# Two products of each key tile of a hybrid RWKV-7 block, moved from VectorE to GpSimd

## The chip, the cores and the metric

The kernel runs on one core of one Trainium2 chip. The metric is the device time of one execution in microseconds (us); the time of a kernel is the median of its runs. The engines are called as in the profile: PE is TensorE's matrix multiplication and PEld its weight load, DVE is VectorE, ACT is ScalarE, POOL is GpSimd, SP is SyncE, which here only issues the loads of weights.

## The reference

One layer for 512 tokens of width 1024: a normalization, one wide projection into three token mixers (a short convolution, a gated linear recurrence, an RWKV-7 time mixing with 16 heads of 64), their gated sum, an output projection, and an MLP with squared ReLU. The change touches the inputs of the RWKV-7 recurrence. Cut to that:

```python
decay = jnp.exp(-jnp.exp(w_log))
a = jax.nn.sigmoid(rwkv_a0[l] + xa @ rwkv_a2[l])
kk = kk / jnp.maximum(jnp.sqrt(jnp.sum(kk * kk, axis=-1, keepdims=True)), 1e-12)
k = k * (1.0 + (a - 1.0) * rwkv_ka[l])
...
def step(state, inp):                      # scanned over the tokens
    r_t, w_t, k_t, v_t, kk_t, a_t = inp
    sa = jnp.einsum('bhvk,bhk->bhv', state, -kk_t)
    state = (state * w_t[:, :, None, :]
             + sa[..., None] * (kk_t * a_t)[:, :, None, :]
             + v_t[..., None] * k_t[:, :, None, :])
    return state, jnp.einsum('bhvk,bhk->bhv', state, r_t)
```

## The kernel before

The recurrence is done by chunks of 64 tokens. Within a chunk the running product P of the decays is taken as an exponential of a running sum, so that the recurrence becomes matrix products of four scaled tensors: kk times P of the token before, the receptance r times P, kk times a over P, and the key k over P. The first two stand side by side in the tile AR, the last two in BK, each with 128 channels on the partitions and, on the free axis, 8 chunks of two times 64 columns. A product into one half of such a tile therefore reads 512 columns and writes 8 blocks of 64 with a gap of 64 between them.

The 1024 channels are 8 key tiles of 128, two (jj = 0, 1) in each of four groups (g). For a group, `krv` does all of this:

- it projects k and r of each tile (`proj`: 24 wide matmuls, the weight split into a rounded part `whi` and a rest `wlo`, the latter a subtraction on VectorE at L105) and mixes each with the token before (`shift`: a ScalarE copy at L326 and a VectorE instruction at L108, into `ks` and `rs`);
- for each tile it takes the norm of kk over a matmul `pn` and a chain of short VectorE instructions (`rsqrt_rows`, tile `rqq`), the running sum (`cum`, a scan on VectorE, L462), P (`PP`, with the view `Pt` one column on; ScalarE, L466) and the inverse 1/P (`pinv`, ScalarE, L469), and then AR and BK (L470 to L478). The scaled key is `kp`;
- it takes two products `rk` of r and kp, splits them into a rounded part and a rest (the rests of the second go to the buffers of `t_` and `pinv`), sums them over the channels of a head with the matmuls `pb` (L500), multiplies by v into `bv`, and transposes v (`pV`, L508).

Temporary tiles come from a pool by tag with one buffer each ("a1" to "a5", "ks", "rs", "PPt"), so the same buffer serves the next tile. In the profile they read `a`, since the number in the name is left out; in the order they carry a number of their own, as in `a_712`. After `krv`, `amat` multiplies BK by AR for each chunk and head (`pA`, L530), masks the results into `AXt` on VectorE, and transposes BK (`pB`, L552).

GpSimd sets a few columns (the first of PP in each chunk, L464) and issues the transfers that carry AR, BK, AXt and others to DRAM and back in the layout that the recurrence needs (`axd`, `rtd` at L490, `bkd`, `mpd` at L852). Its one piece of arithmetic is a product at the end, `x0f` at L1251.

Beside the groups' work runs filler work (`ab`: the other two mixers), woven in by generators: `weave` takes one step of the group's work under a raised priority, then some steps of the filler. Within that, a scheduler of the framework fixes each engine's order when the program is built, from the priorities and from its own estimate of how long instructions take. An engine then runs its list strictly in order, and waits for semaphores. Only instructions marked with `keep_in_program_order` or issued by `pin` are held in the written order. So an edit of one instruction can move others.

Of the kernel before, what the change touches and what calls it, by code (L numbers as in the profile page):

```python
# [99 lines left out]
def block_kernel(ctx, tc, xt, win, par, mulr, sw, wout, w1, w2, fg, cst, eyes, out):  # L100
    nc = tc.nc
    v, ac, gp, pe, sy = nc.vector, nc.scalar, nc.gpsimd, nc.tensor, nc.sync

    def tt(o, a, b, op):
        return v.tensor_tensor(out=o, in0=a, in1=b, op=op)  # L105

    def stt(o, a, s, b, op0, op1):
        return v.scalar_tensor_tensor(out=o, in0=a, scalar=s, in1=b, op0=op0, op1=op1)  # L108
# [4 lines left out]
    MUL, ADD, SUB, MAX = ALU.mult, ALU.add, ALU.subtract, ALU.max  # L113
# [46 lines left out]
    def split(pool, src, tag, rows=slice(0, P), bufs=None):  # L160
        th, tl = tag if type(tag) is tuple else (tag + "h", tag + "l")
        hi = pool.tile([P, S], F32R, tag=th, name=th, bufs=bufs)
        lo = pool.tile([P, S], F32R, tag=tl, name=tl, bufs=bufs)
        ac.copy(hi[rows], src)
        tt(lo[rows], src, f(hi[rows]), SUB)
        return hi, lo
# [24 lines left out]
    def rsqrt_rows(pool, o, ps, low, scale=1.0):  # L191

        w = pool.tile([P, S], F32, tag="rqw", name="rqw")
        q = pool.tile([P, 3, 16], F32, tag="rqq", name="rqq")
        v.transpose(w, ps)
        wv = w.rearrange("p (b j) -> p b j", j=32)[:, :, 0]
        if scale == 1.0:
            v.tensor_scalar(out=q[:, 0], in0=wv, scalar1=low, scalar2=None, op0=MAX)
        else:
            ts2(q[:, 0], wv, scale, low, MUL, ADD)  # L200
        rsqrt(q[:, 0], q[:, 1], q[:, 2])
        v.transpose(o, q[:, 1].unsqueeze(2).to_broadcast([P, 16, 32]))
# [20 lines left out]
    def bv_tile(q, dt=F32):  # L223
        return sp.tile([P, S], dt, tag=f"bv{q}", name="bv" if dt == F32 else "ml", align_bytes=AL)
# [86 lines left out]
    def proj(name):  # L311
        w = load_w(win[CN[name]])
        t = pp.tile([P, S], F32, tag="pp", name="pp")
        for kt in range(KT):
            wh, wl = wslice(w, kt)
            mm3(t, wh, wl, hh[:, kt], hl[:, kt], start=kt == 0, stop=kt == KT - 1)
            if kt % 2 == 1 and kt < KT - 1:
                yield
        return t
# [5 lines left out]
    def shift(pt, mu, omu, o):  # L325
        ac.activation(o, pt, AF.Copy, scale=omu)  # L326
        stt(o[:, 1:], pt[:, 0:S - 1], mu, o[:, 1:], MUL, ADD)
# [8 lines left out]
    def WP(tag, bufs=1):  # L336
        return pk.tile([P, S], F32, tag=tag, name=tag, bufs=bufs)
# [68 lines left out]
    def load_sw(pool, tag, j, a, n):  # L406
        raw = wp.tile([P, 2, P], F32, tag="swr", name="swr", bufs=2)
        sy.dma_start(raw[:, 0:n], sw[j, :, a:a + n])
        hi = pool.tile([P, n, P], F32R, tag=tag + "h", name=tag + "h", bufs=1)
        lo = pool.tile([P, n, P], F32R, tag=tag + "l", name=tag + "l", bufs=1)  # L410
        ac.copy(hi, raw[:, 0:n])
        m = tt(lo, raw[:, 0:n], f(hi), SUB)
        if tag == "swc":
            tc.keep_in_program_order(m)
        return hi, lo

    def c3(t):
        return t.rearrange("p (c t) -> p c t", c=NC)
# [4 lines left out]
    def krv(g, G_):  # L423
        G_.AR = pk.tile([P, 2, NC, 2, L], F32, tag="AR", name="AR")
        G_.BK = pk.tile([P, 2, NC, 2, L], F32, tag="BK", name="BK")
        vs = [p1.tile([P, S], F32, tag=f"v{h}", name=f"v{h}") for h in range(2)]
        for jj in range(2):
            j = 2 * g + jj
            if j == 0:
                ks, rs = k0, r0  # L430
            else:
                ks, rs = WP("ks"), WP("rs")
                t = yield from proj(("k", j))
                shift(t, pv("mu_k", j), dvp(OMK, j), ks)
            sq = WP("a1")
            ac.activation(sq, ks, AF.Square, scale=pv("kk", j))
            sqh, sql = split(pk, sq, "b")
            yield
            if j:
                t = yield from proj(("r", j))  # L440
                shift(t, pv("mu_r", j), dvp(OMR, j), rs)
            swh, swl = load_sw(pk, "swa", j, 0, 2)
            pw = pc.tile([P, S], F32, tag="pu", name="pw")
            pe.matmul(pw, swh[:, 0], lws, start=True, stop=False)
            pe.matmul(pw, swl[:, 0], lws, start=False, stop=True)
            sig = WP("a1")
            ac.activation(sig, pw, AF.Tanh, bias=pv("w0", j), scale=0.5)
            ac.activation(sig, sig, AF.Identity, bias=one[:, 0:1])
            pa = pc.tile([P, S], F32, tag="py", name="pa")
            pe.matmul(pa, swh[:, 1], las, start=True, stop=False)  # L450
            pe.matmul(pa, swl[:, 1], las, start=False, stop=True)
            av = WP("a4")
            ac.activation(av, pa, AF.Tanh, bias=pv("a0", j), scale=0.5)
            yield
            pn = pm.tile([P, S], F32, tag="pm", name="pn")
            pe.matmul(pn, bd, sqh, start=True, stop=False)
            pe.matmul(pn, bd, sql, start=False, stop=True)
            kk = WP("a5")
            rsqrt_rows(pk, kk, pn, 1e-24)
            stt(kk, ks, pv("kk", j), kk, MUL, MUL)  # L460
            cum = WP("a2")
            v.tensor_tensor_scan(out=cum, data0=smk, data1=sig, initial=0.0, op0=MUL, op1=ADD)  # L462
            PP = pk.tile([P, NC, L + 1], F32, tag="PPt", name="PPt")
            gp.memset(PP[:, :, 0:1], 1.0)  # L464
            Pt = PP[:, :, 1:L + 1]
            ac.activation(Pt, c3(cum), AF.Exp, scale=-0.5 * CW)  # L466
            v.tensor_copy(PL[:, g, jj], PP[:, :, L])
            pinv = WP("a3")
            ac.activation(pinv, cum, AF.Exp, scale=0.5 * CW)  # L469
            stt(G_.AR[:, jj, :, 0], c3(kk), -1.0, PP[:, :, 0:L], MUL, MUL)  # L470
            tt(G_.AR[:, jj, :, 1], c3(rs), Pt, MUL)
            t_ = WP("a1")
            stt(t_, av, 1.0, kk, ADD, MUL)
            stt(G_.BK[:, jj, :, 0], c3(t_), 0.5, c3(pinv), MUL, MUL)
            kp = WP("a2")
            ac.activation(kp, av, AF.Identity, scale=pv("ka", j), bias=dvp(OKA, j))
            tt(kp, kp, ks, MUL)
            tt(G_.BK[:, jj, :, 1], c3(kp), c3(pinv), MUL)  # L478

            if jj == 0:  # L480
                rk = [WP(f"rk{h}") for h in range(2)]
            for h in range(2):
                r = slice(64 * h, 64 * h + 64)
                stt(rk[h][64 * jj:64 * jj + 64], rs[r], part[r, PI["rk"], j:j + 1], kp[r], MUL, MUL)

        for jj in range(2):
            for h in range(2):
                gp.dma_start(axd[0, :, 0:64, g, 2 * h + jj].rearrange("c d t -> d c t"),
                             G_.AR[64 * h:64 * h + 64, jj, :, 0])
            gp.dma_start(rtd[:, :, g, jj].rearrange("c p t -> p c t"), G_.AR[:, jj, :, 1])  # L490
        rk = [split(pk, rk[h], ("a1", "a3") if h else "b") for h in range(2)]
        for h in range(2):
            q = 2 * g + h
            t = yield from proj(("v", q))
            shift(t, pv("mu_v", q), dvp(OMV, q), vs[h])
            yield
        for h in range(2):
            pb = pm.tile([P, S], F32, tag="pm", name="pb")
            for i in range(2):
                pe.matmul(pb, bd, rk[h][i], start=i == 0, stop=i == 1)  # L500
            BV[2 * g + h] = bv_tile(2 * g + h)
            tt(BV[2 * g + h], pb, vs[h], MUL)
        yield
        for b in range(2):
            pt = pm.tile([P, 2, 2, P], F32, tag="pm", name="pV")
            for i in range(2):
                for h in range(2):
                    pe.transpose(pt[:, i, h], vs[h][:, (2 * b + i) * P:(2 * b + i + 1) * P], ident)  # L508
            vt = p1.tile([P, 2, 2, P], F32, tag="vt", name="vt", bufs=2)
            ac.copy(vt, pt)  # L510
            for i in range(2):
                c = 2 * (2 * b + i)
                gp.dma_start(vtd[c:c + 2, :, g].rearrange("c s e v -> (c s) (e v)"),
                             vt[:, i].rearrange("p h x -> p (h x)"))
        yield
# [826 lines left out]
```

## Time and profile before

| | |
|---|---|
| median of 3 runs | 1024.95 us (1024.88 to 1027.47) |
| the profiled execution | 1024.48 us |
| its span, first to last instruction | 1022.7 us |
| mean granted clock of TensorE | 0.997 |
| the groups' work (first `pn` to last `pB`) | about 47 to 394 us |
| VectorE busy from 50 to 100 us | 44.80 us |
| VectorE busy from 130 to 190 us | 46.00 us |
| VectorE busy from 250 to 320 us | 52.81 us |
| VectorE busy from 340 to 405 us | 49.32 us |

The profile shows one execution. "Busy" is the time in which an engine worked on an instruction; a wait is the idle time in front of an instruction, put down to the instruction that ended last among those it waited for ("<-"). A row of a timeline has the start in us from the span's start, the length in us, engine, line, operation, tile written and tiles read, and in brackets the idle time before. In a list of waits each row has the waiting instruction, the releaser, the total in us, how often, and the longest. Successive instructions of one engine overlap somewhat, so the distance of their starts is shorter than their lengths: a wide matmul is listed with 0.39 us, and 150 of them between 15 and 50 us took 35.00 us.

### The profile page before, as it was taken

What the parts mean: (1) busy time and instruction counts of PE and PEld (TensorE: products, weight loads), DVE (VectorE), ACT (ScalarE), POOL (GpSimd) and SP (SyncE); (2) the same over time, 40 slices, a digit from 0 to 9 for tenths busy, and PEclk for the clock granted to TensorE, in tenths of its full rate; (3) what the DMA queues carried; (4) which work ended last, traced back from release to release, by engine and by line L of the source; (5) the groups of instructions that cost most, each with busy time, mean ns of one, the idle gap of its engine ahead of it and who ended that gap; (6) DMA issues with size and microseconds to landing.
All of it is one profiled execution on the core that took longest, in us unless ns stands there. A gap on an engine that the chain in (4) does not pass through costs nothing.

```text
span 1022.7 us, 15725 instructions
## 1 busy us (share of the span) xinstructions
PE 1005.3 (98%) x6110; PEld 817.6 (80%) x6110; DVE 735.9 (72%) x1251; ACT 512.7 (50%) x757; POOL 114.0 (11%) x187
## 2 busy tenths in 40 slices
PE   8999999999999999999999999999999999999997
PEld 5777887888887878888887887888888888888885
DVE  6997597599865876795668778646555546987775
ACT  7765463655544655365446444435333334445354
POOL 1012011201212112201222100110000000000001
PEclk9999999999999999999999999999999999999998
DMA  6443744834546445844777634543323324643452
GB/s 233 125 128 107 191 134 116 220 103 130 147 136 165 125 138 147 268 143 129 209 225 212 187 88 120 174 141 127 94 92 104 102 84 171 222 139 128 144 165 103
DMA packets 50266, 151.28 MB, mean 148 GB/s; under 512 B 6672, under 2 KB 10256, under 8 KB 50192
## 3 DMA queue, kind: packets, MB, share of 16 engines
q1 hardware_dynamic: 34816, 99.93, 30.8%
q0 software_dynamic: 14656, 49.29, 17.8%
q8 instruction: 48, 0.79, 0.3%
q10 hardware_dynamic: 720, 1.05, 0.3%
q14 instruction: 26, 0.21, 0.1%
HBM read 123.52 MB, written 26.74 MB: 147 GB/s over the span
## 4 chain that ended last, share of the span: by engine, by line
PE 84%; DVE 9%; ACT 2%; DMA 2%; issue 2%; SPq 0%; DVEq 0%; ACTq 0%
PE acc L1102 16%; PE pp L169 13%; PE pp L171 12%; PE pp L170 12%; PE p L169 6%; PE p L171 6%; PE p L170 6%; DVE wlo L105 2%; PE acc L169 1%; PE acc L171 1%; PE acc L170 1%; DMA raw<-in_win 1%; PE py L688 1%; DMA xT<-in_xt 1%; PE pu L677 1%
## 5 line engine op out<-in xcount | busy, mean ns | idle before, releaser
L148 ACT CAST whi<-raw 128x1024 fp32r<-128x1024 f32 (+1 forms) x164 | 169.6, 1037 | 251.0 <-PE pp L170 76.3
L105 DVE TENSOR_TENSOR wlo<-raw,whi 128x1024 fp32r<-128x1024 f32 (+1 forms) x176 | 206.7, 1176 | 93.6 <-ACT whi L148 93.1
L169 PE MATMUL pp<-hh,whi 128*128 128x512 f32 x688 | 270.6, 394 | 1.1 <-DVE rs L108 1.1
L170 PE MATMUL pp<-hl,whi 128*128 128x512 f32 x688 | 269.8, 392 | 0.0
L171 PE MATMUL pp<-hh,wlo 128*128 128x512 f32 x688 | 269.7, 392 | 0.0
L169 PEld LDWEIGHTS pp<-hh,whi 128*128 128x128 f32 x688 | 129.2, 188 | 29.0 <-DVE rs L108 1.7
L171 PEld LDWEIGHTS pp<-hh,wlo 128*128 128x128 f32 x688 | 129.2, 188 | 27.4 <-DVE wlo L105 0.3
L170 PEld LDWEIGHTS pp<-hl,whi 128*128 128x128 f32 x688 | 129.2, 188 | 26.6
L169 PE MATMUL p<-h2h,whi 128*128 128x512 f32 x256 | 100.4, 392 | 0.0
L171 PE MATMUL p<-h2h,wlo 128*128 128x512 f32 x256 | 99.7, 389 | 0.0
L170 PE MATMUL p<-h2l,whi 128*128 128x512 f32 x256 | 99.7, 389 | 0.0
L108 DVE SCALAR_TENSOR_TENSOR r<-p,rsb 128x512 f32<-128x512 f32 x32 | 22.1, 692 | 69.1 <-PE p L171 68.8
L171 PEld LDWEIGHTS p<-h2h,wlo 128*128 128x128 f32 x256 | 48.1, 188 | 10.1
L170 PEld LDWEIGHTS p<-h2l,whi 128*128 128x128 f32 x256 | 48.1, 188 | 9.8
L169 PEld LDWEIGHTS p<-h2h,whi 128*128 128x128 f32 x256 | 48.1, 188 | 9.6
L1251 POOL TENSOR_TENSOR x0f<-xr,fgt 128x512 f32<-128x512 f32 x4 | 5.2, 1296 | 309.9 <-DMA raw<-in_w 300.8
L170 PE MATMUL acc<-ml,whi 128*128 128x512 f32 x64 | 25.0, 391 | 0.0
L171 PE MATMUL acc<-mh,wlo 128*128 128x512 f32 x64 | 25.0, 390 | 0.0
L1102 PE MATMUL acc<-whi,a2h 128*128 128x512 f32 x64 | 24.9, 389 | 0.0
L1102 PE MATMUL acc<-whi,a2l 128*128 128x512 f32 x64 | 24.9, 389 | 0.0
L1102 PE MATMUL acc<-wlo,a2h 128*128 128x512 f32 x64 | 24.9, 389 | 0.0
L1102 PE MATMUL acc<-whi,ah 128*128 128x512 f32 x64 | 24.9, 389 | 0.0
(369 smaller groups left out, 1741.4 us busy)
## 6 DMA issues: line engine op xcount, KB each, us to landing
raw<-in_win SPq DMA_DIRECT2D x88, 512.0 KB, 3.8
raw<-in_w SPq DMA_DIRECT2D x64, 512.0 KB, 3.6
axd<-AXt POOLq DMA_DIRECT2D x12, 512.0 KB, 8.2
raw<-in_w SPq DMA_DIRECT2D x24, 256.0 KB, 2.8
bkd<-BKT POOLq DMA_DIRECT2D x4, 1024.0 KB, 15.1
ay<-axd POOLq DMA_DIRECT2D x8, 512.0 KB, 6.4
raw<-in_wout SPq DMA_DIRECT2D x8, 512.0 KB, 3.5
bk<-bkd POOLq DMA_DIRECT2D x7, 512.0 KB, 6.1
```

The costliest lines, as they stand in the source:

```text
L105: return v.tensor_tensor(out=o, in0=a, in1=b, op=op)
L108: return v.scalar_tensor_tensor(out=o, in0=a, scalar=s, in1=b, op0=op0, op1=op1)
L148: ac.copy(hi[:, sl], raw[:, sl])
L169: pe.matmul(ps, wh, xh, start=start, stop=False)
L170: pe.matmul(ps, wh, xl, start=False, stop=False)
L171: pe.matmul(ps, wl, xh, start=False, stop=stop)
L677: pin(n, lambda: pe.matmul(pu[64 * h:64 * h + 64, x], ax[rows, g, e], sv[rows, g, e], start=True, stop=True))
L688: pin(behind, lambda: pe.matmul(py[64 * h:64 * h + 64, x], w, y, start=first and x == 0, stop=last, skip_group_check=True))
L1102: pe.matmul(b[i], x_[:, ms], w_, start=id(b[i]) not in begun, stop=last and n == 2, skip_group_check=True)
L1251: gp.tensor_tensor(out=o0, in0=x0, in1=fgt[0], op=MUL)
```

## The change

Of the four products of a key tile, the one of r and P (into AR, L471) and the one of kp and 1/P (into BK, L478) are issued on GpSimd instead of VectorE. Operands, results and everything else in the code are the same.

```diff
@@ -468,14 +468,14 @@
             pinv = WP("a3")
             ac.activation(pinv, cum, AF.Exp, scale=0.5 * CW)
             stt(G_.AR[:, jj, :, 0], c3(kk), -1.0, PP[:, :, 0:L], MUL, MUL)
-            tt(G_.AR[:, jj, :, 1], c3(rs), Pt, MUL)
+            gp.tensor_tensor(out=G_.AR[:, jj, :, 1], in0=c3(rs), in1=Pt, op=MUL)
             t_ = WP("a1")
             stt(t_, av, 1.0, kk, ADD, MUL)
             stt(G_.BK[:, jj, :, 0], c3(t_), 0.5, c3(pinv), MUL, MUL)
             kp = WP("a2")
             ac.activation(kp, av, AF.Identity, scale=pv("ka", j), bias=dvp(OKA, j))
             tt(kp, kp, ks, MUL)
-            tt(G_.BK[:, jj, :, 1], c3(kp), c3(pinv), MUL)
+            gp.tensor_tensor(out=G_.BK[:, jj, :, 1], in0=c3(kp), in1=c3(pinv), op=MUL)
```

There are 16 such products, two for each of the 8 key tiles. On GpSimd they stand in the queue of transfers. This is the piece of the difference for the first group's two tiles; `ISA` is an instruction that sets GpSimd up for arithmetic, `Z<-in_eyes` a transfer that comes earlier:

```order
 L563 DMA Z<-in_eyes 128x1024
+L471 ISA
+L471 TENSOR_TENSOR AR<-rs,PPt 128x8x64
 L490 DMA rtd<-AR 128x8x64
+L478 TENSOR_TENSOR BK<-a_503,a_496 128x8x64
 L464 MEMSET PPt 128x8
 L488 DMA axd<-AR 64x8x64 x2
+L471 TENSOR_TENSOR AR<-rs,PPt 128x8x64
 L490 DMA rtd<-AR 128x8x64
+L478 TENSOR_TENSOR BK<-a_696,a_689 128x8x64
 L488 DMA axd<-AR 64x8x64 x2
 L464 MEMSET PPt 128x8
```

Each product stands where its tile's first transfer is, with the rtd transfer between the two. The ISA row stood in front of x0f before.

The scheduler also orders VectorE anew around the products. In the first group's second tile, before, VectorE's rows from `bv` to the rest of the second rk product (`a_713`) are these; `BK<-a_693,a_689` is BK's first half, `wlo` are weight rests for the filler:

```order
L105 TENSOR_TENSOR bv<-pb,v_431 128x512
L202 STREAM_TRANSPOSE a_666<-rqq 128x512
L105 TENSOR_TENSOR wlo<-raw,whi 128x1024
L108 SCALAR_TENSOR_TENSOR a_666<-ks,part,a_666 128x512
L105 TENSOR_TENSOR wlo<-raw,whi 128x1024
L108 SCALAR_TENSOR_TENSOR AR<-a_666,PPt 128x8x64
L108 SCALAR_TENSOR_TENSOR a_693<-a_654,a_666 128x512
L108 SCALAR_TENSOR_TENSOR u_729<-u_729,g_580 128x512
L108 SCALAR_TENSOR_TENSOR BK<-a_693,a_689 128x8x64
L105 TENSOR_TENSOR a_713<-rk_508,a_712 128x512
```

And after:

```order
L202 STREAM_TRANSPOSE a_666<-rqq 128x512
L105 TENSOR_TENSOR a_696<-a_696,ks 128x512
L108 SCALAR_TENSOR_TENSOR a_666<-ks,part,a_666 128x512
L108 SCALAR_TENSOR_TENSOR rk_507<-rs,part,a_696 64x512
L108 SCALAR_TENSOR_TENSOR AR<-a_666,PPt 128x8x64
L108 SCALAR_TENSOR_TENSOR a_693<-a_654,a_666 128x512
L108 SCALAR_TENSOR_TENSOR rk_508<-rs,part,a_696 64x512
L108 SCALAR_TENSOR_TENSOR BK<-a_693,a_689 128x8x64
L105 TENSOR_TENSOR bl<-rk_507,bh 128x512
L108 SCALAR_TENSOR_TENSOR v_432<-pp,part,v_432 128x511
L105 TENSOR_TENSOR a_713<-rk_508,a_712 128x512
L105 TENSOR_TENSOR bv<-pb,v_431 128x512
```

Two `wlo`, `bv` and `u_729` that stood ahead of BK's first half now stand behind it, and so do `bl` and `v_432`, which before came ahead of `bv`. In the first tile of this group the instruction `a_473<-ks,part,a_473`, which stood behind `rs`, now stands ahead of it. In the second group, one `wlo` that stood ahead of BK's first half stands behind.

On TensorE the readers of those results move with them. In the second group, for the matmuls `pb` of the second rk product, the piece of the difference is:

```order
 L500 MATMUL pb<-bl,bd 128x512
 L500 MATMUL pb<-a_1425,bd 128x512
-L169 MATMUL pp<-hh,whi 128x512
-L170 MATMUL pp<-hl,whi 128x512
-L171 MATMUL pp<-hh,wlo 128x512
-L169 MATMUL pp<-hh,whi 128x512
 L500 MATMUL pb<-a_1426,bd 128x512
+L169 MATMUL pp<-hh,whi 128x512
```

The second `pb` comes four wide matmuls earlier. In the first group the move is larger: counted from the program's start, the pb of `a_712` is preceded by 309 wide matmuls before and by 283 after, that of `a_713` by 310 and 288. In the third and fourth group TensorE's order is the same, and so is SP's everywhere.

## The prediction

> **What bounds the kernel now.** I read the page first (busy shares), then TensorE's waits, then the chain of waits and the timelines around the places where TensorE stops, and last the only GpSimd products that the kernel has, near its end.
>
> ```profile
> PE 1005.3 (98%) x6110; PEld 817.6 (80%) x6110; DVE 735.9 (72%) x1251; ACT 512.7 (50%) x757; POOL 114.0 (11%) x187
> ```
>
> TensorE is busy for 98% of the span, so VectorE time as such is worth nothing: only what shortens or lengthens a stop of TensorE counts. These are the stops in the stretch where the change lies (50 to 400 us), from the list of TensorE's waits:
>
> ```profile
> PE pB L552 <- DVE AXt L105: 1.5, 2, 1.2
> PE pV L508 <- DVE bv L105: 1.2, 1, 1.2
> PE pp L169 <- DVE rs L108: 1.1, 1, 1.1
> PE pb L500 <- ACT a L164: 1.0, 1, 1.0
> PE pb L500 <- ACT bh L164: 0.4, 1, 0.4
> ```
>
> They sum to 5.2 us, which is the most that any edit of VectorE's work there can win: 0.5% of the time.
>
> **What the change removes and adds.** The rows of the two products on VectorE (from the queries for their tiles AR and BK), and the page's row of the one product that GpSimd already does on a tile of the same size:
>
> ```profile
> L105 DVE TENSOR_TENSOR AR<-rs,PPt x8: 680/684/691, 52.2 to 359.2; 128x512 f32<-128x512 f32 x8
> L105 DVE TENSOR_TENSOR BK<-a,a x8: 651/685/692, 55.0 to 363.2; 128x512 f32<-128x512 f32 x8
> L1251 POOL TENSOR_TENSOR x0f<-xr,fgt 128x512 f32<-128x512 f32 x4 | 5.2, 1296 | 309.9 <-DMA raw<-in_w 300.8 <-DVE xr L105 4.2 <-ACT fj L1250 3.5
> ```
>
> Sixteen products leave VectorE. Successive VectorE instructions overlap a little, so one product gives back about 0.60 us of its 0.685 (the chain below has it as 0.59 and 0.60), 1.20 us per key tile. GpSimd takes 1.30 us for one, 1.9 times as long, 2.6 us per key tile and 20.7 us in all on an engine that is 11% busy.
>
> Are these products on the path to a stop? The chain of waits, in order of time (start, length, what), says so for group 0, for group 1 and for group 3:
>
> ```profile
> 52.27 0.59 DVE AR L105
> 55.04 0.60 DVE BK L105
> 60.87 0.64 DVE rs L108
> 61.55 0.50 PE pp L169
> ...
> 149.29 0.60 DVE AR L105
> 152.02 0.60 DVE BK L105
> 161.51 0.63 ACT a L164
> 162.18 0.50 PE pb L500
> 163.37 0.23 PE pp L169
> ...
> 359.32 0.59 DVE AR L105
> 363.31 0.57 DVE BK L105
> 377.75 0.70 DVE bv L105
> 378.49 0.66 PE pV L508 x4
> ```
>
> In group 0 the two products stand in the run of VectorE work that ends in rs, for which TensorE stops at 61.55. In groups 1 and 3 they stand in the runs that end in the pb and pV stops. In group 2 the stop is pB's for AXt, behind pA, where the products have long been read, and I give it no change.
>
> **What the moved products cost elsewhere.** First as waiting. GpSimd's queue is idle where the products come: the product of rs waits for the exponential on ScalarE, the second for kp, and the nearest reader, pA, comes late: in group 0, the densest, the second tile's product of kp starts at 74.07 and pA at 90.06 (VectorE's and TensorE's timelines).
>
> ```profile
> 74.07 0.69 DVE L105 TENSOR_TENSOR BK<-a,a 128x512 f32<-128x512 f32 x1
> 90.06 1.19 PE L530 MATMUL pA<-AR,BK 64*128 64x128 f32 x15
> ```
>
> So the extra 0.6 us of each, and the 0.9 us of the rtd transfer's issue between them, reach nobody; if that cover were gone they would cost about 1.5 us a tile. The same holds for the writers that now wait for GpSimd (the next scan into kp's buffer, the split into the inverse decay's, the next shift into rs). The ISA row that moves from GpSimd's last product to its first stands here:
>
> ```profile
> 36.15 0.58 POOL L563 DMA_DIRECT2D Z<-in_eyes  x1 [21.21 <-PE r L171]
> 53.29 0.91 POOL L490 DMA_DIRECT2D rtd<-AR  x1 [16.56 <-DVE spt L397]
> ```
>
> It has 16.56 us of idle time to itself, as it had 300.8 before x0f. No row shows its length, so I bound it by these: nothing up to 16.56 us, and past that only the cover of the first pA. I cost it at nothing.
>
> Second, as company. This is the term that decides. The timelines of GpSimd and VectorE at the end of the program show the two engines side by side:
>
> ```profile
> 996.26 1.29 POOL L1251 TENSOR_TENSOR x0f<-xr,fgt 128x512 f32<-128x512 f32 x1 [300.79 <-DMA raw<-in_w]
> 997.11 1.53 DVE L105 TENSOR_TENSOR wlo<-raw,whi 128x1024 fp32r<-128x1024 f32 x1 [0.89 <-ACT whi L148]
> 998.98 1.30 POOL L1251 TENSOR_TENSOR x0f<-xr,fgt 128x512 f32<-128x512 f32 x1 [1.42 <-PE acc L1102]
> 999.83 1.53 DVE L105 TENSOR_TENSOR wlo<-raw,whi 128x1024 fp32r<-128x1024 f32 x1 [1.19 <-ACT whi L148]
> 1002.50 1.23 DVE L105 TENSOR_TENSOR wlo<-raw,whi 128x1024 fp32r<-128x1024 f32 x1 [1.15 <-ACT whi L148]
> 1003.69 2.49 DVE L105 TENSOR_TENSOR xr<-acc,xr 128x512 f32<-128x512 f32 x4
> 1004.52 1.29 POOL L1251 TENSOR_TENSOR x0f<-xr,fgt 128x512 f32<-128x512 f32 x1 [4.24 <-DVE xr L105]
> 1009.29 1.29 POOL L1251 TENSOR_TENSOR x0f<-xr,fgt 128x512 f32<-128x512 f32 x1 [3.48 <-ACT fj L1250]
> 1009.81 0.69 DVE L105 TENSOR_TENSOR xr<-acc,xr 128x512 f32<-128x512 f32 x1 [1.02 <-PE acc L1102]
> ```
>
> A wlo that starts alone takes 1.23 us. The two that start 0.44 us before the end of a GpSimd product take 1.53: held for 0.30. The xr additions, which read one operand from PSUM, are not held by the third and fourth product. So a VectorE instruction with both inputs in SBUF is held until about 0.14 us before the product's end. In the new places VectorE has hardly a gap and most of its instructions read two SBUF tensors. Call k the hold on VectorE per product: at least 0 (GpSimd gives way), at most 1.30 - 0.14 = 1.16 (a VectorE instruction arrives just behind every product's start). The four products above show 0.30, 0.30, 0 and 0, mean 0.15, but with VectorE half idle. I take the middle between 0.15 and 1.16, k = 0.65, because VectorE is denser there than at the end and yet runs transposes, PSUM readers and short instructions in between. The break-even of VectorE's own time is k = 0.60.
>
> The Trainium skill, SBUF — State Buffer, section Who interferes with whom, says that of such a VectorE instruction and a GpSimd instruction that reads SBUF the one that issues second is blocked fully until the first ends. The two held wlo agree with it (0.30 of 0.44 us). By that rule alone the sum below would be its upper end.
>
> **What the new order does.** The order around the stops moves too. These rows of the timelines carry it, two of group 0's second key tile and three of group 1's:
>
> ```profile
> 84.82 0.62 ACT L164 CAST a<-rk 128x512 fp32r<-128x512 f32 x1 [3.12 <-DVE BK L108]
> 85.77 0.40 PE L500 MATMUL pb<-a,bd 128*128 128x512 f32 x1
> ...
> 161.39 1.22 DVE L105 TENSOR_TENSOR wlo<-raw,whi 128x1024 fp32r<-128x1024 f32 x1
> 162.53 0.68 DVE L105 TENSOR_TENSOR a<-rk,a 128x512 fp32r<-128x512 f32 x1
> 163.44 0.39 PE L500 MATMUL pb<-a,bd 128*128 128x512 f32 x1
> ```
>
> In group 0, second key tile, TensorE asks for the split products of rk (a_712, a_713) 26 wide matmuls earlier, 26 x 0.23 = 6.0 us by the pitch of the pp row at 163.37. VectorE's way to BK's first half, which the cast at 84.82 waits for, is shortened by the two products (1.20), two wlo moved behind it (161.39 to 162.53: 1.14 each) and bv, bl, v and u moved behind it (about 0.62 each): 6.0 us. So with k = 0 it is just in time (before, the cast ended 0.33 us ahead of the matmul at 85.77), and any hold shows in full.
>
> **The sum**, against the profiled execution's own 1024.48 us (span 1022.7), which lies 0.47 below the median 1024.95:
> - Group 0, stop for rs (1.11): -1.20 for two products, +0.64 because another instruction of rs's size now stands ahead of rs, +2k. With k = 0: -0.56; 0.65: +0.74; 1.16: +1.76.
> - Group 0, second tile: 2k less the slack of 0.33: 0, +1.0, +2.0. (The 0.4 us for bh stays.)
> - Group 1: the first pb gains 1.20 + 1.14 (a wlo moved behind BK), capped at its 0.95 us. The second pb, which started at 163.44 on a split that ended at 163.21, is asked for four matmuls (0.92) earlier, and 0.95 more by the first one's gain: at 161.57. The split ends at 163.21 - 2.34 + 2k. Together: -0.95, -0.35, +0.65.
> - Group 2: 0.
> - Group 3, stop for bv (1.22): -1.20 + 2k: -1.2, +0.1, +1.1.
>
> With k = 0 this is -2.7 us, with 0.65 +1.5, with 1.16 +5.5. Everything before 50 us and after 400 us keeps its order on TensorE, and the weight loads on SP theirs, so I add nothing for it. From the median: 1022.2, **1026.4**, 1030.5 us.
>
> **Rivals.**
> 1. *Full hold* (slower): each of the products, when its turn comes, holds the next VectorE instruction for 1.16 us, so a key tile gains 1.20 and loses 2.32. For it: the held wlo, and the density of VectorE in group 0. Against it: VectorE's readers of PSUM and its transposes aren't held. 1030.5 us; it decides from k of about 0.85 on. This is also what the rule of the page named above gives.
> 2. *No hold* (GpSimd gives way and fits its products into VectorE's gaps): GpSimd has 16 us for a pair, so its own delay is free. -2.7 us, 1022.2. If the stops in all groups but one also closed, the 5.2 us of the list less group 2's 1.2 would bring 1021.0, which would count as faster.
> 3. *GpSimd late*: its queue is in order, and a product behind a transfer that waits (mpd for g) would hold pA. Against it: the mpd transfers stand ahead of the next product's inputs in the order of before too, and pA has 16 us of slack. If one group's pA waited 3 us for it, the time would be 1026.4 + 3 = 1029.4; it decides once a product is 16 + 1.6 us late (1.6 us lead from the forecast to 1028.0).
>
> **How the numbers follow.** A measurement of this kernel can tell about 0.3% (3.1 us) from no change, so faster means under 1021.9 and slower over 1028.0. Partial hold (k from 0.2 to 0.85, my forecast): 0.50. Full hold: 0.27. No hold: 0.19, of which 0.08 reaches faster. GpSimd late: 0.04. So faster 0.08, same 0.61, slower 0.31. The range runs from the no-hold sum to the full-hold sum, 1022.2 to 1030.5, with 0.1 left out at each end.
>
> **What would show it.** Right: 16 products of about 1.3 us on GpSimd; VectorE instructions beside them stretched, by 0.65 us per product on average; stops of TensorE in group 0 up by 1 to 2 us, those of groups 1 and 3 no longer. Wrong: GpSimd's products stretched instead and VectorE's not (rival 2), a pA that waits for GpSimd (rival 3), or a change of TensorE's time outside 50 to 400 us, for which I have no mechanism.

## The result and the profile after

The change made the kernel slower: 1044.07 us, median of 6 runs (1040.29 to 1046.72), beside 1024.81 us (1023.89 to 1027.47) for the kernel before. The ratio is 1.0179, interval 1.0163 to 1.0195. The forecast was 1026.4 us with a range up to 1030.5; the time lies 13.6 us above its upper end. The profiled execution is the fastest of the six, 1040.29 us with a span of 1038.5 us, 15.8 us longer than before.

The page's row of busy times after:

```profile
PE 1009.4 (97%) x6110; PEld 820.0 (79%) x6110; DVE 744.2 (72%) x1235; ACT 512.2 (49%) x757; POOL 137.5 (13%) x203
```

VectorE has 16 instructions fewer, which took 10.9 us before (16 x 0.684), and yet is busy for 8.3 us more. TensorE does the same 6110 matmuls, in 4.1 us more. Both are explained below. The list of TensorE's waits between 40 and 410 us (total, times, longest):

```profile
PE pV L508 <- DVE bv L105: 3.1, 2, 2.1
PE pp L169 <- DVE rs L108: 2.9, 1, 2.9
PE pp L169 <- ACT g L793: 2.5, 1, 2.5
PE pb L500 <- ACT bh L164: 2.5, 1, 2.5
PE pB L552 <- DVE AXt L105: 2.3, 3, 1.2
PE pp L171 <- DVE wlo L105: 2.2, 1, 2.2
PE pb L500 <- DVE a L105: 0.6, 1, 0.6
PE pw L445 <- DVE swal L105: 0.5, 1, 0.5
PE pb L500 <- ACT a L164: 0.5, 1, 0.5
```

With a last row of 0.2 for `bl` that makes 17.3 us, against 5.2 before in the five rows of the prediction. Every one of the long stops is for VectorE or for a ScalarE instruction that waits for VectorE; none is for GpSimd. GpSimd's own products, from its groups by form, are 16, of 23.5 us in all, where the prediction had 20.7.

```profile
L478 POOL TENSOR_TENSOR BK<-a,a 128x512 f32<-128x512 f32 x8 | 13.0, 1626 | 12.6 <-DVE a L105 10.4 <-DVE rqq L108 2.2
L471 POOL TENSOR_TENSOR AR<-rs,PPt 128x512 f32<-128x512 f32 x8 | 10.5, 1317 | 92.5 <-ACT PPt L466 92.5
```

What they do to VectorE is seen in the timelines of GpSimd, VectorE and TensorE. Group 3, first key tile, after, in order of time (start, length, what):

```profile
351.31 0.17 DVE L467 COPY PL<-PPt 128x8 f32<-128x8 f32 x1
351.36 1.19 POOL L471 TENSOR_TENSOR AR<-rs,PPt 128x512 f32<-128x512 f32 x1 [23.46 <-ACT PPt L466]
351.39 1.19 DVE L108 SCALAR_TENSOR_TENSOR rqq<-rqq 128x16 f32<-128x16 f32 x1
352.62 0.71 DVE L202 STREAM_TRANSPOSE a<-rqq 128x512 f32<-128x512 f32 x1
...
354.63 0.69 DVE L108 SCALAR_TENSOR_TENSOR AR<-a,PPt 128x512 f32<-128x512 f32 x1
354.87 1.59 POOL L478 TENSOR_TENSOR BK<-a,a 128x512 f32<-128x512 f32 x1 [0.98 <-DVE a L105]
355.24 1.77 DVE L108 SCALAR_TENSOR_TENSOR a<-a,a 128x512 f32<-128x512 f32 x1
356.93 1.21 DVE L105 TENSOR_TENSOR wlo<-raw,whi 128x1024 fp32r<-128x1024 f32 x1
...
358.20 0.50 PE L171 MATMUL pp<-hh,wlo 128*128 128x512 f32 x1 [2.18 <-DVE wlo L105]
```

A step of the norm on 128x16 numbers, 0.18 us elsewhere, takes 1.19 us: it starts 0.03 us behind the first product and ends 0.03 us after it. The second product meets `AR` on VectorE and takes 1.59 us, where the shortest product into BK took 1.30; the next VectorE instruction, `a`, waits in turn and takes 1.77 instead of 0.69. The weight rest `wlo` behind it comes 2 us late, and TensorE stands still for 2.18 us. This holds for all 16 products: each stretches exactly one VectorE instruction, by 0.88 to 1.11 us, together 16.3 us (summed over the VectorE rows beside a product, against the same rows where no product runs). What is met may be short: 9 of the 16 have 8 or 16 columns (six two-input steps of the norm, one step with one input, two copies `PL`), the other 7 read two tensors of 512 columns. No transposition and no reader of PSUM stood next behind a product's start, so this kernel says nothing on those. In group 0 this is VectorE's row of a step of the norm with one input, before:

```profile
52.03 0.17 DVE L111 TENSOR_SCALAR rqq<-rqq 128x16 int32<-128x16 int32 x1
```

and after, beside the first product of the program:

```profile
51.69 1.17 DVE L111 TENSOR_SCALAR rqq<-rqq 128x16 int32<-128x16 int32 x1
```

VectorE's account closes with the kernel of the experiments that has neither the products on VectorE nor a hold: it is busy for 728.1 us, and 728.1 + 16.3 = 744.4, beside 744.2 measured.

### The profile page after: what moved, and what is told of

Its sections match the earlier page's. It is cut to its first block, busy times and chain, and to the rows that moved or that the text cites. A ratio compares the mean times of both kernels' runs of the same rounds, so it can differ in the third digit from the quotient of the medians.

```text
span 1038.5 us, 15729 instructions
## 1 busy us (share of the span) xinstructions
PE 1009.4 (97%) x6110; PEld 820.0 (79%) x6110; DVE 744.2 (72%) x1235; ACT 512.2 (49%) x757; POOL 137.5 (13%) x203
## 4 chain that ended last, share of the span: by engine, by line
PE 69%; DVE 10%; issue 3%; DMA 3%; ACT 2%; POOL 0%; ACTq 0%; DVEq 0%; POOLq 0%
PE acc L1102 11%; PE pp L169 10%; PE pp L171 10%; PE pp L170 10%; PE p L171 6%; PE p L170 6%; PE p L169 6%; DVE wlo L105 2%; DMA raw<-in_w 2%; PE acc L171 1%; PE acc L170 1%; PE acc L169 1%; PE py L688 1%; ACT whi L148 1%; PE pA L530 1%
```

## The experiments

All kernels of the first batch ran on one chip beside the kernel before (1025.16 us, 15 runs), those of the second beside 1025.12 us (7 runs), those of the third beside 1025.3 us (9 runs).

**The change once more**, without an edit.

> The changed kernel once more, in the same rounds as the controls. Its first profile shows each of the 16 products holding one VectorE instruction for 0.9 to 1.1 us, TensorE stops that are 12 us longer in sum, and two stretches of 3.4 us at half the TensorE clock (2 x 1.7 us lost). If stops near 2 us or longer halve the clock, and how often depends on where they fall, this profile has another number of such stretches than two, and a time that goes with it, about 1.7 us per stretch; the median stays 1040 to 1047.

Measured: 1042.6 us (1042.17 to 1045.68), ratio 1.0174 (1.0155 to 1.0193). The number of stretches at half clock between 50 and 400 us is two again, at the same stops; the other number that the expectation spoke of did not come.

**The products only written.** GpSimd sets the two halves to a constant instead of computing the products:

```diff
-gp.tensor_tensor(out=G_.AR[:, jj, :, 1], in0=c3(rs), in1=Pt, op=MUL)
+gp.memset(G_.AR[:, jj, :, 1], 0.5)
-gp.tensor_tensor(out=G_.BK[:, jj, :, 1], in0=c3(kp), in1=c3(pinv), op=MUL)
+gp.memset(G_.BK[:, jj, :, 1], 0.5)
```

> As the changed kernel, with TensorE's, ScalarE's and SP's order exactly its own, but GpSimd only fills the two halves with a constant (it leaves the two products out) and so reads nothing. Theory hold: the loss is VectorE being held by GpSimd's reads; without them VectorE has 16 x 0.60 us less to do, no instruction of VectorE is held, and the time is 1020 to 1024. Rival order: the new order asks for results earlier than they come, whatever GpSimd does; then 1030 or more.

Measured: 1025.47 us (1024.74 to 1027.89), ratio 1.0003 (0.9993 to 1.0012). The 16 instructions are on GpSimd at 0.53 us each. They wait for no input, so they run at other times than the products, in pairs or fours (at 15 to 17, 97, 106, 179, 207, 310 and 320 us). VectorE instructions with two inputs run beside them there, and none is longer than elsewhere; for instance two `u`, 0.75 us each:

```profile
205.83 1.22 DVE L105 TENSOR_TENSOR wlo<-raw,whi 128x1024 fp32r<-128x1024 f32 x1
206.76 1.01 POOL L478 MEMSET BK<- 128x512 f32 x2
206.97 1.53 DVE L108 SCALAR_TENSOR_TENSOR u<-u,part,u 128x511 f32<-128x511 f32 x2
```

TensorE's waits between 40 and 410 us are short again:

```profile
PE pB L552 <- DVE AXt L105: 2.3, 3, 1.2
PE pp L169 <- DVE rs L108: 0.8, 1, 0.8
PE pp L169 <- ACT g L793: 0.6, 1, 0.6
PE pb L500 <- ACT bh L164: 0.6, 1, 0.6
PE pb L500 <- DVE bl L105: 0.2, 1, 0.2
```

Two things follow. The slow-down is not the new order, which this kernel shares on TensorE, ScalarE and SyncE; it needs the products themselves, which read, run longer and run beside the groups' work. And the relief itself, 10.9 us of VectorE's work gone (its busy time falls by 7.8 us) and nothing put in its place, brings no gain that the times show: the stops for `bv` (1.2) and `a` (1.0) of before went, and `AXt` (+0.8), `g` (+0.6) and some tenths came, because TensorE, no longer stopped at one place, arrives earlier at the next.

**The products as copies.** GpSimd copies one input in place of multiplying two:

```diff
+gp.tensor_copy(G_.AR[:, jj, :, 1], c3(rs))
+gp.tensor_copy(G_.BK[:, jj, :, 1], c3(kp))
```

> As the changed kernel, all engines' orders exactly its own but for GpSimd's, where each product is a copy of one of its two operands (the other factor is left out). Theory hold by the shared read path: a copy reads one tensor and should take less than a product's 1.3 us, and VectorE is held for about as long as the copy runs less 0.14 us: held sum between 0 and 16 us, time between that of the fill and that of the change, near 1030. Rival, that only a two-input GpSimd instruction holds VectorE: time as with the fill.

Measured: 1028.8 us (1027.06 to 1029.56), ratio 1.0032 (1.0019 to 1.0044). The copies take 0.92 us on average, and 11 of the 16 stretch a VectorE instruction, by 0.23 to 0.42 us, 3.9 us in sum. So a GpSimd instruction with one input holds VectorE too. That its holds are fewer and shorter can't be put to the one input alone: the copies of `rs` do not wait for the exponential and so run earlier than the products, and the five that held nothing (0.61 us each) all ran beside the transposition of `pn` out of PSUM, which had started before them.

**The products beside VectorE's own.** The kernel before, with the same two products done once more on GpSimd into a tile that nobody reads, so that VectorE is not relieved and every other engine's order is that of before (settings of the priority are left out of the cut, here and below):

```diff
 tt(G_.AR[:, jj, :, 1], c3(rs), Pt, MUL)
+jk = pk.tile([P, NC, L], F32, tag="jk", name="jk", bufs=1)
+gp.tensor_tensor(out=jk, in0=c3(rs), in1=Pt, op=MUL)
 tt(G_.BK[:, jj, :, 1], c3(kp), c3(pinv), MUL)
+gp.tensor_tensor(out=jk, in0=c3(kp), in1=c3(pinv), op=MUL)
```

> The kernel before, every order but GpSimd's unchanged, with the 16 products computed on GpSimd a second time into a tile that nobody reads. Nothing is taken off VectorE. Theory hold: 16 holds of about 1.0 us, VectorE later by up to 16 us in the groups' runs, TensorE stops longer by more than in the changed kernel, 1040 or more. Rival order: the holds are absorbed where the order is the old one; 1025 to 1030.

Measured: 1044.34 us (1042.37 to 1044.9), ratio 1.0181 (1.0165 to 1.0197): the whole loss of the change, with nothing moved and nobody waiting for GpSimd. Each of the 16 holds one VectorE instruction, 16.4 us in sum; TensorE's waits between 40 and 410 us sum to 17.4 us, much as in the changed kernel. The first one, from the timelines of this kernel, holds the same step of the norm as in the changed kernel:

```profile
52.86 1.42 POOL L471 TENSOR_TENSOR jk<-rs,PPt 128x512 f32<-128x512 f32 x1 [15.03 <-ACT PPt L466]
53.15 1.17 DVE L111 TENSOR_SCALAR rqq<-rqq 128x16 int32<-128x16 int32 x1
54.30 0.68 DVE L105 TENSOR_TENSOR AR<-rs,PPt 128x512 f32<-128x512 f32 x1
```

**One product of the two**: the AR product alone on GpSimd, and the BK product alone; the other goes back to `tt`. In these two the scheduler fixed the orders of TensorE, ScalarE and VectorE anew, so that they are neither those of before nor those of the change.

> Only the AR product (receptance by decay) is taken on GpSimd; the BK product stays on VectorE. Theory A (each product holds one VectorE instruction for about 1.02 us, and the hold falls on the chain TensorE waits for): in the changed kernel the stops grew by 12.8 us over those of the kernel that only wrote, 0.8 us for each of 16 products, so 8 products give about +6.4 us: 1031.5 us, 1029 to 1033, and since a stop grows by only one hold, no stretch at half clock. Rival B (each tile can absorb one hold, and only the second one of a tile stops TensorE): no more than 1027 us.

Measured: 1033.04 us (1032.56 to 1033.34), ratio 1.0072 (1.0057 to 1.0087), at the top of what theory A gave, with 8 holds, 8.1 us in sum. One stretch at half clock came too, which the expectation excluded.

> Only the BK product (key part by inverse decay) is taken on GpSimd. Theory A: as for the AR product alone, 8 holds of about 1.02 us, 1029 to 1033 us, no half clock. Rival B: 1027 us or less. If A holds and the losses add, this one's loss and that of the AR product alone make about 13 us, and what is left to the 17.6 us of both is the half clock.

Measured: 1031.84 us (1031.4 to 1032.9), ratio 1.0062 (1.0047 to 1.0077), 8 holds, 8.0 us in sum, no half clock between 50 and 400 us. The rival, a first hold that a tile absorbs, falls with both: the stops for `rs`, `bh` and `wlo`, 0.8, 0.6 and 0.1 us in the kernel that only writes, are 1.7, 1.7 and 1.1 with the AR product and 1.5, 1.5 and 1.0 with the BK product, about one hold more. The two losses, 7.9 and 6.7 us, make 14.6 of the 17 to 19 us of the whole.

**The products in halves**: each as two instructions of four chunks.

```diff
+for q_ in range(2): gp.tensor_tensor(out=G_.AR[:, jj, 4 * q_:4 * q_ + 4, 1],
+    in0=c3(rs)[:, 4 * q_:4 * q_ + 4], in1=Pt[:, 4 * q_:4 * q_ + 4], op=MUL)
```

(and the same for BK).

> The changed kernel with each product issued as two GpSimd instructions of four chunks, 32 in all; every other engine's order as in the changed kernel. Theory A (a VectorE instruction that meets a GpSimd product waits until that instruction ends; VectorE then gets one instruction in before the second half): two holds of about 0.5 us for each product, about 16 us in sum as before, 1040 to 1046 us. Rival B (a handover costs a fixed 1 us whatever its length): 32 holds of 1.0 us, over 1055 us. Rival C (short instructions fall into VectorE's gaps): under 10 us of holds, about 1033 us.

Measured: 1038.74 us (1037.47 to 1040.48), ratio 1.0129 (1.0113 to 1.0145). 31 VectorE instructions are held, by 0.35 to 0.55 us, 14.6 us in sum; the time is 1.3 us below the bottom of what theory A gave. A hold is as long as what is left of the GpSimd instruction, not a fixed price; VectorE gets one instruction in between. The one half that holds nothing is met by a transposition. These are the two halves of an AR product of group 3 in one row, the second from 355.51 to 356.19 us, and what VectorE runs beside them:

```profile
354.85 1.33 POOL L471 TENSOR_TENSOR AR<-rs,PPt 128x256 f32<-128x256 f32 x2 [23.44 <-ACT PPt L466]
354.88 0.69 DVE L108 SCALAR_TENSOR_TENSOR rqq<-rqq 128x16 f32<-128x16 f32 x1
355.60 0.71 DVE L202 STREAM_TRANSPOSE a<-rqq 128x512 f32<-128x512 f32 x1
```

The step of the norm waits for the first half; the transposition, which starts inside the second, takes its usual 0.71 us.

Over these kernels the loss follows the holds:

| | holds | sum of holds, us | time less before, us |
|---|---|---|---|
| only written | 0 | 0 | 0.3 |
| copies | 11 | 3.9 | 3.6 |
| BK alone | 8 | 8.0 | 6.7 |
| AR alone | 8 | 8.1 | 7.9 |
| halves | 31 | 14.6 | 13.6 |
| the change (second run) | 16 | 16.3 | 17.4 |
| beside | 16 | 16.4 | 19.2 |

**Why the last two lose more than they are held.** In some stretches of the trace TensorE's granted clock is 0.5 instead of 1.0. Between 50 and 400 us they are 3.41 us long (once 6.83), begin on a fixed grid of 3.41 us, and follow a long stop. There is one in the kernel with the AR product alone and one in that of the halves; the kernel with the products beside VectorE's own has two of 3.41 us and the one of 6.83. In the changed kernel there are two, behind the stops of group 3 (windows of the trace: length, PE, PEld, DVE, ACT and POOL busy, granted clock, DMA share, GB/s):

```profile
356.00:363.00 7.00, 4.82 (x15) 3.81 (x15) 6.97 (x9) 0.30 (x1) 1.87 (x4) 0.76 0.65 177
363.00:390.00 27.00, 27.00 (x120) 22.21 (x119) 22.07 (x37) 14.18 (x21) 5.81 (x6) 1.00 0.31 91
390.00:397.00 7.00, 4.91 (x19) 3.78 (x19) 3.07 (x5) 2.00 (x4) 2.20 (x4) 0.76 0.67 204
```

To see whether idle time brings them, two kernels fill part of the stops. In `mm3`, chosen calls repeat their second matmul, which stands in TensorE's queue directly ahead of the stop; the calls around the second stop are held in the written order, and the other engines' orders are unchanged (on TensorE, besides the repeats, one matmul moved by a few places, and in the second kernel two). Cut to the repeats:

```diff
         pe.matmul(ps, wh, xl, start=False, stop=False)
+        for _ in range({419: 6, 458: 6}.get(n, 0)):     # n: how many mm3 calls so far
+            pe.matmul(ps, wh, xl, start=False, stop=False)
```

> The changed kernel with six repeats of one matmul (adding its product six times more, so that this sum isn't the reference's) in TensorE's queue ahead of each of the two long stops of the last group, at 355.6 and 390.1 us in the changed kernel; each six take about 1.36 us of a stop of 2.1 us that is idle otherwise. Theory A (idle time within one clock stretch of 3.41 us is what brings half clock): no stretch at half clock after these two stops, and as each cost about 1.7 us, about 3 us less than the changed kernel: 1039 to 1040 us. Rival B (the half clock comes from the load or from something else): both stretches stay, 1042 to 1045 us.

Measured: 1042.15 us (1041.65 to 1043.33), ratio 1.0162 (1.0145 to 1.0179). Both stretches are gone, as theory A says, but the time is not 1039 to 1040: in this run the stop of group 2, 3.15 us long instead of 2.52, met the grid so that most of it lay in one stretch (2.72 us idle in it) and brought a half clock there, which the changed kernel's own trace does not have. So that stop was filled as well, by eight repeats (`346: 8`), beside a third run of the changed kernel:

> The kernel with repeats of one matmul ahead of the two long stops of group 3, and eight more ahead of the long stop of group 2 (292.4 us in the changed kernel; 1.82 us of its 2.5), so three sums are not the reference's. Theory A (idle time within one clock stretch brings half clock): no stretch at half clock in groups 2 and 3, and what is left of the loss is the holds' own 12.8 us: 1037 to 1040 us, some 3 us less than the changed kernel beside it. Rival B (half clock has another cause and moves on to another place, or the repeats cost what they save): within 1.5 us of the changed kernel beside it.

> The changed kernel once more, beside the kernel with all long stops filled: 1041 to 1044 us, with one to three stretches at half clock between 50 and 400 us (both theories).

Measured: 1040.93 us (1040.12 to 1043.75), ratio 1.0158 (1.0143 to 1.0173), beside 1042.31 us (1041.14 to 1046.39), ratio 1.0178 (1.0159 to 1.0197). As times the two cannot be told apart: the 1.4 us are what rival B allows. The traces can. With the stops filled the same two windows read

```profile
356.00:363.00 7.00, 6.16 (x28) 4.74 (x27) 6.99 (x9) 2.12 (x4) 3.21 (x5) 1.00 0.50 122
390.00:397.00 7.00, 6.29 (x32) 4.87 (x31) 3.79 (x5) 2.71 (x5) 2.17 (x4) 1.00 0.60 187
```

and the lateness of TensorE against the kernel before, taken at the first `pn` of groups 0 to 3 and at the first `pB` of group 3, grew group by group by (us, from the starts of these matmuls):

| | group 0 | group 1 | group 2 | group 3 |
|---|---|---|---|---|
| only written | 0.8 | -1.7 | 0.8 | -1.0 |
| the change, three traces | 4.5, 4.9, 4.7 | 2.4, 2.3, 2.3 | 2.7, 2.7, 2.7 | 6.4, 6.4, 6.4 |
| two stops filled | 4.9 | 2.3 | 4.9 | 3.3 |
| three stops filled | 6.4 | 2.3 | 2.9 | 3.4 |

In group 3 filling took away 3.0 to 3.1 us, in both kernels alike. But where no half clock had been, one came: in group 2 of the first (+2.2), in group 0 of the second (+1.7, behind the unfilled stop for `rs`). Which stop is hit depends on how the grid lies to the program in that execution. This is why the time of the filled kernels did not fall as I expected, and it was my omission to leave group 0's stops unfilled. That the half clock behind the stops of group 3 follows from their idle time is shown; that the kernel would run at 1039 us without any is not.

## Why the prediction was wrong

Two steps of the sum failed, and the clock was not in it. TensorE came to the first `pB` of group 3 later by 16.0 us, counted from the first `pn` (the table above); the forecast had +1.5.

**The hold per product, k.** I took 0.65 us between bounds of 0 and 1.16; it is 1.02 (16.3 / 16). What failed in this term is that short and one-input instructions would run beside a product without being held, and that there would be enough such instructions. A one-input step on 128x16 and a copy of 128x8 (`PL`, L467) were held for 1.0 us like the rest, and since VectorE's queue is strictly in order, it is enough that the *next* instruction can be held. The other half of the argument, transpositions and readers of PSUM, was not refuted: in the changed kernel none stood in that place, and the one transposition that did, in the kernel of the halves, was not held. What I drew from the end of the kernel (0.15 us on average) came from places where VectorE arrives late or reads PSUM. By size this is the smaller failure: k = 1.02 in place of 0.65 takes my sum from +1.5 to +4.4 us, and even the upper bound gave no more than +5.5. The Trainium skill, SBUF — State Buffer, section Who interferes with whom, says that whoever issues second is blocked until the other ends; my text took it for the upper end, and the traces agree with it almost fully (1.02 of products of 1.2 to 1.4 us). The same section lists copies and tensor-scalar instructions among those that can take the shared ports, and says that a GpSimd instruction that only writes does not contend with VectorE's two-input reads; here the copy was held for 1.0 us, and beside 16 memsets nothing was. I had looked at neither in the terms of my sum.

**The places.** This is the larger failure: I let the holds count only at the stops that the kernel before had, and each less a gain. Of the 16.0 us, 4.4 are covered by my sum with the measured k, about 3.1 are the clock, and the remaining 8.5 lie here. With k = 1.02 my own sum gives +4.4 us: 3.2 in group 0, 0.4 in group 1, nothing in group 2, 0.8 in group 3. The table above has 4.5 to 4.9, 2.3, 2.7 and 6.4, together 16. Against the kernel that only writes, which has the same order on TensorE, the stop of five of the eight tiles grew by just about the tile's two holds:

| tile | TensorE waits for | only written | after | grew by | its two holds |
|---|---|---|---|---|---|
| group 0, first | rs | 0.82 | 2.91 | 2.09 | 1.00 + 1.09 |
| group 0, second | bh | 0.61 | 2.46 | 1.84 | 1.01 + 0.88 |
| group 2, second | g (ScalarE) | 0.64 | 2.52 | 1.88 | 1.02 + 0.92 |
| group 3, first | wlo | 0.13 | 2.18 | 2.05 | 1.02 + 1.09 |
| group 3, second | bv | 0.03 | 2.09 | 2.07 | 1.01 + 1.11 |

In group 1 the two tiles have no such single stop. TensorE's lateness over the group grew by 4.0 us against the kernel that only writes, for four holds of 4.2; the stops that came there, for `swal`, twice `a`, and `bv`, sum to 2.6 us, of which my sum had only those for `a`, and the rest I can't put to a stop. In group 2 the first tile's two holds, 2.0 us, reached nobody: TensorE has no stop between 255 and 295 us.

My sum had the first and the last of the table, and the second by its size, though at the rests `a` behind `bh`. It gave group 2 nothing, and in group 3 looked only at `bv` at the end of the chain: I had read which waits existed before, and not which chains stood just behind TensorE with a few tenths of slack. The weight rests `wlo`, which are filler for VectorE, are such a chain. Group 2 shows how far a hold reaches; this is the end of its chain of waits after (start, length, what):

```profile
288.71 1.68 DVE rk L108
...
292.52 0.70 DVE BK L108
...
293.25 0.02 ACT a L164
...
293.77 1.04 ACT whi L148
294.81 0.49 ACT g L793
```

The held `rk` delays `BK`'s first half, which reads the buffer that the cast `a` overwrites; the cast now stands in ScalarE's queue ahead of a weight cast and of `g`, neither of which depends on it, and TensorE waits for `g`. The new place of the cast was to be read from ScalarE's order, which I had not followed.

**The gains.** I credited every stop with the 1.20 us that two products give back (-2.7 us in all with k = 0). The kernel that only writes shows no such gain: its ratio is 1.0003, and in its trace TensorE gained 1.0 us from the first `pn` to the first `pB` of group 3. Only part of the credit was wrong at its place: the stops for `bv` and `a` did vanish. But 0.8 and 0.6 us came back at `AXt` and `g`.

**The clock** I had not reckoned with at all: some 3 us in the changed kernel, in two stretches.

So with the mean hold the account of TensorE's time between the first `pn` and the first `pB` of group 3, changed kernel against only written, is 17.0 us: about 3.1 of half clock in group 3 and 13.9 of waiting, which is 85% of the 16.3 us of holds. Of the 2.4 us that are missing, 2.0 are the two holds of group 2's first tile.

**The rivals.** Rival 1, the full hold, is the mechanism that happened, with 0.27 against 0.50 for the partial one, but its price, 1030.5, still lay 13.6 us below the measured time, because it was worked out at the same few places. Rival 2, no hold, did not happen. Rival 3, GpSimd late, did not happen: `pA` never waited for it, and the product's own length, the transfer between the two and the setup row cost nothing, as I had it. The order outside 50 to 400 us stayed as forecast: of the 15.8 us, 15.6 had been lost by the first `pB` of group 3.

## What to carry to other kernels

Before work is moved from VectorE to GpSimd, price the move as nearly the GpSimd instruction's whole length taken out of VectorE (here 1.02 us of about 1.2), once per instruction, wherever VectorE's queue is dense; a 0.69 us product moved to a 1.2 us one on the other engine is then a loss even if nobody waits for its result. Price the gain by asking what the bounding engine waits for next: where it is 98% busy, taking 11 us off the second engine may bring nothing at all. And list not only the waits that exist but the chains that arrive just in time, through every in-order queue on the way, since a delay of one microsecond turns each of them into a stop.

## What I had not expected of the hardware

- The clock went to half after less idle time than one whole stretch. Over the traces of all twelve kernels and repeats, with TensorE's idle time summed by stretches of 3.41 us, none with up to 1.76 us was followed by half clock between 40 and 1000 us, and all from 1.83 us on were (up to 2.83); between them, at 1.80 and 1.81, it went both ways. The Trainium skill, TensorE: Matmul & The Clock Gate, section What's actually happening, has the free-running window of 3413 ns and puts the fall at an idle window of about 3.4 us; the window agrees with the grid of the traces, but half a window of idle time was enough here.
- A stop of 2.9 us at 59.7 us in the changed kernel left the clock alone because it lay across two stretches; the same stop brought half clock in two other kernels. Whether this also makes the times of one kernel differ (1040.29 to 1046.72 for the changed one) is not shown: its three traces, of executions of 1040.29, 1042.66 and 1042.13 us, all have two stretches between 50 and 400 us.
- GpSimd is held as well as VectorE: its products took from 1.17 to 1.76 us in the changed kernel, and the one at 354.87 us that met `AR` on VectorE 1.59.
